# Layer 1's attention scores as three float32r products of 64 rows, two heads on the two halves of the array, in place of stacked parts

## The chip, the cores and the metric

The kernel runs on one core of a Trainium2 chip. The metric is the device time of one execution in microseconds, the lower the better. The engines are TensorE (PE in the profile, its weight loads PEld), VectorE (DVE), ScalarE (ACT), GpSimd (POOL) and SyncE (SP), which here issues the weight transfers.

## The reference, cut to what matters

Four blocks run over 256 tokens of width 1024: layer 0 (two kinds of attention, then an MLP), layer 1 (forgetting attention, then an MLP), an mLSTM mixer and a sparse-attention mixer. The change touches the forgetting attention, 16 heads of 64:

```python
def forgetting_attention(q, k, v, log_f):
    c = jnp.cumsum(log_f, axis=1)
    ...
        s = jnp.einsum("bqhd,bshd->bhqs", qb, k).astype(jnp.float32) * scale
        s = s + jnp.transpose(cq, (0, 2, 1))[..., None] - c_k[:, :, None, :]
        s = jnp.where((key_pos[None, :] <= t[:, None])[None, None], s, -jnp.inf)
        p = jax.nn.softmax(s, axis=-1)
        return jnp.einsum("bhqs,bshd->bqhd", p.astype(v.dtype), v)
```

The term of the query position cancels in the softmax, so the kernel adds only the term of the key position, `-c`.

## The kernel before, in words

**Precision.** A float32 value is cut into a high part, rounded to float32r (ACT writes it), and a low part, the remainder (DVE writes it). A product is then three float32r products: high by high, high by low, low by high. The weights are cut the same way as they arrive from memory (`cut`, L118 on ACT and L121 on DVE), and the big products are L174 to L176 (tokens on the output's partitions) and L213 to L216 (features on the partitions).

**Layer 1** (`layer1`) works in two groups of eight heads. For each it makes q, k and v (`gemm_tok`), normalises each head (`head_norm`), transposes q and k two head pairs at a time (L382) into a tile `t`, and hands four pairs to `causal_heads`. The products of the second group's q, k, v stand in the program behind the first group's attention, and the first half of `out_proj` behind the second group's, so that TensorE has other products to do while a softmax runs.

**Stacked parts.** With 64 features a head fills half of the 128 rows that a product sums over. `stack_queries` puts a head's high part on its own half of the partitions and its low part on the other half. `stack_keys` makes two arrangements of each key head, so that two products of 128 rows (L468) hold all four products of parts. A stacked head takes five instructions on TensorE: two products for each of the two blocks of query rows (128 and 256 keys wide), and one of 384 columns (L482) that adds `-c`, held as high and low rows in `negc`. Each head has a PSUM bank of its own (`banks`; two buffers of one bank).

**Layer 0** computes its scores with plain float32 operands of 64 rows: head 0 of a pair lies on partitions 0 to 63, head 1 on 64 to 127, and the products of the two alternate. Its two banks are one tile with one buffer, from the pool `p0`, which closes when layer 0 ends; the pool `pr` with the two separate banks opens then.

**Softmax** (`softmax`): four reads of the score banks by DVE (L425, two for each head), the exponentials on ACT (L428), the scaling on DVE (L443). Then TensorE transposes the weights (L455), copies follow (L457), and `pv` multiplies by v (L491). A pair's scores are asked for before the pair ahead of it is finished.

**Order.** The order of each engine's instructions is laid down by a planner when the program is built; only inside a `manual_schedule` block does TensorE keep the order as written. At run time an engine takes its instructions in that order, each waiting for its semaphores, and everything behind it on that engine waits too.

Of the kernel before, what the change touches and what calls it, by code (L numbers as in the profile page):

```python
# [16 lines left out]
P = 128  # L17
# [22 lines left out]
class Cols:  # L40
# [11 lines left out]
    def fill(self, arrays):  # L52
        out = np.zeros((P, self.n), np.float32)
        for k, a in arrays.items():
# [8 lines left out]
CST = Cols(ident=128, causal=256, mlmask=256, gmask=32, gsum=16, gsum2=48, cc=32, ss=32, cmp=30, any=2, rmask=8,  # L63
           sel=16)
# [11 lines left out]
class Builder:  # L76
# [384 lines left out]
    def scores(self, qs, kss, extra=None):  # L461
# [3 lines left out]

        def one(e, c, t0, w):
            for i, k in enumerate(kss[e]):
                nc.tensor.matmul(ss[e][:, c:c + w], qs[e][:, t0:t0 + P], k[:, :w], start=c == 0 and i == 0,  # L468
                                 stop=extra is None and c > 0 and i == len(kss[e]) - 1)

        places = ((0, 0, P), (P, P, 2 * P))
        if len(kss[0]) == 1:
            with self.tc.manual_schedule(engines={PE}):
                for place in places:
                    for e in range(2):
                        one(e, *place)
        else:
            for e in range(2):
                for place in places:
                    one(e, *place)  # L480
                if extra is not None:
                    nc.tensor.matmul(ss[e][:, :384], extra[e][0], extra[e][1], start=False, stop=True)  # L482
# [11 lines left out]
    def causal_heads(self, pool, qk, v, vcol, tables, yh, yl, npair, extra=None, sinks=None):  # L494
        def weights(p):
            pairs = [qk(p, e) for e in range(2)]
            s = self.scores([q for q, _ in pairs], [ks for _, ks in pairs],
                            [extra(2 * p + e) for e in range(2)] if extra else None)
# [14 lines left out]
    def layer0(self):  # L513
        nc, tc = self.nc, self.tc
        hg = VEC(self.vec, "hg")
        with tc.tile_pool(name="l0", bufs=2) as pool:
# [14 lines left out]
            half = lambda t, e: t[64 * e:64 * e + 64]  # L531
# [17 lines left out]
            self.causal_heads(pool, lambda p, e: (half(qT[:, 4 + p], e), [half(kT[:, 4], e)]), kv, lambda p, e: 128 + e * 64,  # L549
# [7 lines left out]
            self.causal_heads(pool, lambda p, e: (half(qT[:, p], e), [half(kT[:, p], e)]), v, lambda p, e: (2 * p + e) * 64,  # L557
# [5 lines left out]
    def layer1(self):  # L563
        nc, tc = self.nc, self.tc
        hg = VEC(self.vec, "hg")
        with tc.tile_pool(name="l1", bufs=2) as pool:
# [8 lines left out]
            nc.vector.memset(negc.bitcast(F32), 0.0)  # L575
            causal = CST(self.cst, "causal")

            def forget():
                row = self.rstd_row()
                parts = gates()  # L580
                o = self.pa.tile([P, 512], F32, name="t", tag="t", bufs=PSUM["t"])[:16, :T]
                nc.tensor.matmul(o, CST(self.cst, "gsum"), parts, start=True, stop=True)
                f = pool.tile([16, T], F32, name="f", tag="f", bufs=1)
                a = pool.tile([16, T], F32, name="fa", tag="fa", bufs=1)
                nc.vector.tensor_tensor(f, o, row[:16], op=ALU.mult)
                nc.vector.tensor_scalar(f, f, VEC(self.vec, "bf")[:16], None, op0=ALU.add)
                self.log_sigmoid(f, a)
                one = pool.tile([16, T], F32, name="fone", tag="fone", bufs=1)
                nc.vector.memset(one, 1.0)
                c = pool.tile([16, T], F32, name="fc", tag="fc", bufs=1)  # L590
# [735 lines left out]
```

## Time and profile before

| | us |
|---|---|
| three runs, median (lowest to highest) | 950.76 (949.65 to 953.34) |
| the profiled execution | 949.85 |
| its span of instructions | 947.7 |
| PE busy | 929.6 |
| DVE busy | 701.0 |
| ACT busy | 567.4 |

Busy time is the sum of the instruction records of an engine within the span. A record of TensorE lasts longer than the step to the next one, since products are pipelined, so the start-to-start step tells what an instruction takes of the engine, and a short gap does not show as idle time. The 2.1 us between the execution's time and its span lie around the instructions.

### The profile page before, as it was taken

To read this page: it belongs to the slowest core of one execution; us is meant where nothing else is said; L and a number is where in the kernel's file an instruction comes from. 1 tells how busy PE (TensorE), PEld (TensorE's weight loads), DVE (VectorE), ACT (ScalarE), POOL (GpSimd) and SP (SyncE) were. 2 spreads that over 40 slices of the span, in tenths; PEclk is the share of its full clock that TensorE was granted. 3 is DMA by queue.
4 is the path that set the end of the run, shared out by engine and by line. 5 is a ranking of instruction groups with operands and counts; after the bars stand their busy time and mean duration, and the time that the engine had idled before them with its cause. 6 is when DMAs were issued, how large, how long until landed. Compare 5 with 4: busy or idle time off the path is not lost.

```text
span 947.7 us, 17580 instructions
## 1 busy us (share of the span) xinstructions
PE 929.6 (98%) x7068; PEld 850.6 (90%) x7068; DVE 701.0 (74%) x1521; ACT 567.4 (60%) x1048; POOL 6.8 (1%) x16
## 2 busy tenths in 40 slices
PE   8999999999999999999999999999999999999997
PEld 6777999999998778899999999999888998888986
DVE  6997866655556897998665555988688778678994
ACT  7767655543445786865554444555645456379883
POOL 0000000000000000000000000000000000000000
PEclk9999999999999999999999999999999999999999
DMA  8723555555655334265555555545221555341311
GB/s 306 295 93 132 180 184 198 193 179 185 208 187 185 129 117 149 86 225 181 200 199 180 200 199 189 185 151 187 91 90 46 178 192 178 134 178 46 112 46 44
DMA packets 22608, 152.52 MB, mean 161 GB/s; under 512 B 2608, under 2 KB 2736, under 8 KB 4992
## 3 DMA queue, kind: packets, MB, share of 16 engines
q1 hardware_dynamic: 21744, 148.43, 44.9%
q0 software_dynamic: 784, 2.98, 0.9%
q8 instruction: 55, 0.90, 0.4%
q14 instruction: 25, 0.20, 0.1%
HBM read 150.36 MB, written 1.05 MB: 160 GB/s over the span
## 4 chain that ended last, share of the span: by engine, by line
PE 85%; ACT 7%; DVE 5%; issue 1%; DMA 1%; SPq 0%; ACTq 0%; DVEq 0%
PE g L213 19%; PE g L215 19%; PE g L216 19%; PE g L174 4%; PE g L175 3%; PE g L176 3%; PE o L491 2%; PE t L455 2%; ACT whi L118 2%; DVE wlo L121 1%; PE s L1058 1%; ACT kst L409 1%; DVE kst L411 1%; PE s L468 1%; PE o L828 1%
## 5 line engine op out<-in xcount | busy, mean ns | idle before, releaser
L121 DVE TENSOR_TENSOR wlo<-wraw,whi 128x1024 fp32r<-128x1024 f32 (+1 forms) x274 | 324.3, 1203 | 138.3 <-ACT whi L118 137.7
L118 ACT ACTIVATE whi<-wraw 128x1024 fp32r<-128x1024 f32 (+1 forms) x274 | 277.9, 1041 | 222.6 <-PE g L215 121.6
L213 PE MATMUL g<-xh,whi 128*128 128x256 f32 x928 | 260.9, 281 | 0.4 <-ACT nqr L1010 0.4
L216 PE MATMUL g<-xh,wlo 128*128 128x256 f32 x928 | 261.0, 281 | 0.0
L215 PE MATMUL g<-xl,whi 128*128 128x256 f32 x928 | 260.6, 281 | 0.5 <-DVE xl L254 0.5
L213 PEld LDWEIGHTS g<-xh,whi 128*128 128x128 f32 x928 | 174.4, 188 | 4.1 <-issue 3.0
L216 PEld LDWEIGHTS g<-xh,wlo 128*128 128x128 f32 x928 | 175.7, 189 | 0.6
L215 PEld LDWEIGHTS g<-xl,whi 128*128 128x128 f32 x928 | 174.6, 188 | 1.2 <-DVE xl L254 0.7
L216 PE MATMUL g<-hh,wlo 128*128 128x256 f32 x512 | 141.5, 276 | 0.0
L213 PE MATMUL g<-hh,whi 128*128 128x256 f32 x512 | 141.5, 276 | 0.0
L215 PE MATMUL g<-hl,whi 128*128 128x256 f32 x512 | 141.3, 276 | 0.0
L213 PEld LDWEIGHTS g<-hh,whi 128*128 128x128 f32 x512 | 96.1, 188 | 0.0
L215 PEld LDWEIGHTS g<-hl,whi 128*128 128x128 f32 x512 | 96.1, 188 | 0.0
L216 PEld LDWEIGHTS g<-hh,wlo 128*128 128x128 f32 x512 | 96.1, 188 | 0.0
L174 PE MATMUL g<-whi,xh 128*128 128x512 f32 x192 | 76.4, 399 | 2.4 <-DVE E L929 1.6
L175 PE MATMUL g<-wlo,xh 128*128 128x512 f32 x192 | 75.9, 395 | 0.0
L176 PE MATMUL g<-whi,xl 128*128 128x512 f32 x192 | 75.7, 396 | 0.0
L216 PE MATMUL g<-yh,wlo 128*128 128x256 f32 x224 | 63.3, 283 | 0.0
L213 PE MATMUL g<-yh,whi 128*128 128x256 f32 x224 | 63.2, 284 | 0.0
L215 PE MATMUL g<-yl,whi 128*128 128x256 f32 x224 | 63.2, 283 | 0.0
L428 ACT ACTIVATE L<-L,nm 128x128 f32<-128x128 f32 (+1 forms) x128 | 56.8, 450 | 6.8 <-DVE nm L425 6.5
L174 PEld LDWEIGHTS g<-whi,xh 128*128 128x128 f32 x192 | 36.1, 188 | 12.8 <-ACT xh L253 2.6
(348 smaller groups left out, 1396.7 us busy)
## 6 DMA issues: line engine op xcount, KB each, us to landing
wraw<-in_w SPq DMA_DIRECT2D x135, 1024.0 KB, 4.9
wraw<-in_w SPq DMA_DIRECT2D x4, 512.0 KB, 7.3
tabs<-in_tabs SPq DMA_DIRECT2D x2, 1024.0 KB, 8.3
xT<-in_x SPq DMA_DIRECT2D x4, 256.0 KB, 7.4
bdv<-in_bdv POOLq DMA_DIRECT2D x8, 128.0 KB, 4.7
mlw<-in_mlw POOLq DMA_DIRECT2D x1, 992.0 KB, 5.2
nq<-in_gf POOLq DMA_DIRECT2D x1, 512.0 KB, 6.6
out_y<-nqr SPq DMA_DIRECT2D x2, 256.0 KB, 2.1
```

The source lines that it names most:

```text
L118: self.nc.scalar.activation(hi[:, s], w[:, s], AF.Copy)
L121: self.nc.vector.tensor_tensor(lo[:, s], w[:, s], hi[:, s].bitcast(F32), op=ALU.subtract)
L174: nc.tensor.matmul(ps[b][:, :n], xh, hi[:, sl], start=kt == 0, stop=False)
L175: nc.tensor.matmul(ps[b][:, :n], xh, lo[:, sl], start=False, stop=False)
L176: nc.tensor.matmul(ps[b][:, :n], xl, hi[:, sl], start=False, stop=kt == KT - 1)
L213: nc.tensor.matmul(o, hi[:, s], ah, start=bank["new"], stop=False)
L215: nc.tensor.matmul(o, hi[:, s], al, start=False, stop=False)
L216: nc.tensor.matmul(o, lo[:, s], ah, start=False, stop=last and j == 1 and i == len(acts) - 1)
L409: nc.scalar.activation(dst[64 * o:64 * o + 64, :, e, o], ps[own], AF.Copy, scale=sc)
L428: nc.scalar.activation(Ls[i][:, c], Ls[i][:, c], AF.Exp, bias=nm[:, b, i:i + 1], scale=-1.0, accum_out=den[:, b, i:i + 1])
L455: nc.tensor.transpose(ps[:, e, j * P:(j + 1) * P], Ls[e][:, i * P:(i + 1) * P], self.ident)
L491: nc.tensor.matmul(o[64 * e:64 * e + 64, kt * P:T], v[:, kt, c0[e]:c0[e] + 64], pts[kt][:, e], start=start and kt == 0, stop=stop and kt == 1)
```

## The change

Layer 1 no longer stacks. `to_parts` writes the high part of a transposed q or k with one ACT instruction over 128 partitions and the low part with one DVE instruction. `scores` takes a list of terms, for layer 1 (high q, low k), (low q, high k), (high q, high k), and for layer 0 the one float32 term as before. For every term it issues the products of 64 rows of head 0 and head 1 in turn, then one product of 384 columns and 64 rows for each head that adds `-c`, all in one `manual_schedule` block. The product of the two low parts, which the stacked form had, is left out.

The forget gates are computed on 128 partitions, four copies of 16 rows, instead of 16, so that both halves of the partitions hold the high and the low rows of `c`. Layers 0 and 1 and both their MLPs now run inside the pool `p0`, so layer 1 gets the one tile of two banks; `pr` opens before the mLSTM.

```diff
-    def scores(self, qs, kss, extra=None):
+    def scores(self, terms, extra=None):
         nc = self.nc
         ss = self.banks()
...
+        half = lambda t, e: t[64 * e:64 * e + 64]
+        with self.tc.manual_schedule(engines={PE}):
+            for i, (q, k) in enumerate(terms):
+                for c, t0, w in ((0, 0, P), (P, P, 2 * P)):
                     for e in range(2):
+                        nc.tensor.matmul(ss[e][:, c:c + w], half(q, e)[:, t0:t0 + P], half(k, e)[:, :w],
+                                         start=c == 0 and i == 0, stop=extra is None and c > 0 and i == len(terms) - 1)
+            if extra is not None:
+                for e in range(2):
+                    nc.tensor.matmul(ss[e][:, :384], half(extra[e][0], e), half(extra[e][1], e), start=False, stop=True)
         return [(s[:, :P], s[:, P:384]) for s in ss]
...
+    def to_parts(self, dst, t, c0, scale=None):
+        nc = self.nc
+        ps = self.transposed(t, c0, dst.shape[2])
+        hi = dst[:, 0].bitcast(F32)
+        if scale is None:
+            self.split(dst[:, 0], dst[:, 1], ps)
+        else:
+            nc.scalar.activation(dst[:, 0], ps, AF.Copy, scale=scale)
+            nc.vector.scalar_tensor_tensor(dst[:, 1], ps, scale, hi, op0=ALU.mult, op1=ALU.subtract)
...
-            nc.vector.memset(negc.bitcast(F32), 0.0)
+            gsum = pool.tile([P, P], F32, name="gsum", tag="gsum", bufs=1)
+            nc.vector.tensor_copy(gsum.rearrange("p (a b) -> p a b", b=32),
+                                  CST(self.cst, "gsum").unsqueeze(1).to_broadcast([P, 4, 32]))
...
+                hi = pool.tile([P, T], F32R, name="fhi", tag="fhi", bufs=1)
+                nc.scalar.activation(hi, c, AF.Copy, scale=-1.0)
                 for a, w in ((0, P), (P, T)):
-                    nc.scalar.activation(negc[:16, a:a + w], c[:, :w], AF.Copy, scale=-1.0)
-                    nc.vector.scalar_tensor_tensor(negc[32:48, a:a + w], c[:, :w], -1.0, negc[:16, a:a + w].bitcast(F32),
-                                                   op0=ALU.mult, op1=ALU.subtract)
+                    nc.vector.scalar_tensor_tensor(negc[:, a:a + w], hi[:, :w].bitcast(F32), CST(self.cst, "lorow"), c[:, :w],
+                                                   op0=ALU.mult, op1=ALU.add)
...
-                    self.stack_queries(qst[-1], q, p * P)
-                    kst.append(late(pool, [2, 2, 2, T], f"kst{p}"))
-                    self.stack_keys(kst[-1], k, p * P, gk)
+                    self.to_parts(qs[-1], q, p * P)
+                    ks.append(late(pool, [2, 2, T], f"kst{p}"))
+                    self.to_parts(ks[-1], k, p * P, gk)
+                def terms(p):
+                    (qh, ql), (kh, kl) = ([t[p // 2][:, i, p % 2] for i in range(2)] for t in (qs, ks))
+                    return [(qh, kl), (ql, kh), (qh, kh)]
...
             with tc.tile_pool(name="p0", bufs=1, space=bass.MemoryType.PSUM) as self.p0:
-                self.layer0()
+                for s in (self.layer0, lambda: self.mlp(2), self.layer1, lambda: self.mlp(4)):
+                    s()
             with tc.tile_pool(name="pr", bufs=2, space=bass.MemoryType.PSUM) as self.pr:
-                for s in (lambda: self.mlp(2), self.layer1, lambda: self.mlp(4), self.mlstm, self.nsa):
+                for s in (self.mlstm, self.nsa):
```

## Rows read from the trace of the kernel before

**Rows 1.** The page's busy times: us, share of the span, instructions.

```profile
PE 929.6 (98%) x7068; PEld 850.6 (90%) x7068; DVE 701.0 (74%) x1521; ACT 567.4 (60%) x1048; POOL 6.8 (1%) x16
```

**Rows 2.** Windows: length, then busy us (instructions) of PE, PEld, DVE, ACT, POOL.

```profile
36.00:70.50 34.50, 34.50 (x198) 25.60 (x197) 32.01 (x100) 24.91 (x63) 0.00 (x0) 1.00 0.36 125
70.50:110.00 39.50, 38.54 (x318) 34.05 (x317) 31.79 (x87) 28.91 (x73) 0.00 (x0) 1.00 0.42 141
300.00:321.00 21.00, 21.00 (x106) 16.35 (x105) 15.66 (x34) 13.93 (x21) 0.00 (x0) 1.00 0.29 100
321.00:357.00 36.00, 33.55 (x194) 25.66 (x193) 32.70 (x82) 31.16 (x68) 0.00 (x0) 1.00 0.42 147
372.00:405.00 33.00, 31.36 (x250) 28.03 (x249) 30.36 (x81) 26.72 (x63) 0.00 (x0) 1.00 0.36 129
```

**Rows 3.** Timeline of TensorE in layer 1: start, us, instructions, idle time before.

```profile
324.74 0.39 PE L175 MATMUL g<-wlo,xh 128*128 128x512 f32 x1
325.71 0.33 PE L468 MATMUL s<-kst,qst 128*128 128x128 f32 x1 [0.58 <-DVE kst L411]
...
334.84 0.39 PE L175 MATMUL g<-wlo,xh 128*128 128x512 f32 x1
336.04 0.70 PE L468 MATMUL s<-kst,qst 128*128 128x128 f32 x4 [0.81 <-DVE nm L425]
...
336.76 0.62 PE L468 MATMUL s<-kst,qst 128*128 128x128 f32 x4
337.21 0.34 PE L482 MATMUL s<-negc,selr 128*128 128x384 f32 x1
337.38 0.39 PE L176 MATMUL g<-whi,xl 128*128 128x512 f32 x1
...
401.95 0.28 PE L215 MATMUL g<-yl,whi 128*128 128x256 f32 x1
402.26 0.87 PE L491 MATMUL o<-pt,v 128*64 128x256 f32 x8
```

**Rows 4.** Groups by line and shape, 285 to 413 us: count | busy, mean ns | idle before.

```profile
L411 DVE SCALAR_TENSOR_TENSOR kst<-t,gk,kst 64x512 fp32r<-64x512 f32 x16 | 12.0, 749 | 2.3 <-ACT kst L409 1.9
L409 ACT ACTIVATE kst<-t,gk 64x512 fp32r<-64x512 f32 x16 | 10.9, 683 | 1.0 <-PE t L382 0.7
...
L468 PE MATMUL s<-kst,qst 128*128 128x128 f32 x32 | 6.7, 280 | 2.7 <-DVE nm L425 1.9 <-DVE kst L411 0.8
...
L425 DVE CUSTOM_DVE_ANT_0 L<-s,cst 128x256 f32<-128x256 f32 x16 | 6.6, 415 | 0.0
...
L398 DVE TENSOR_TENSOR qst<-t,qst 64x512 fp32r<-64x512 f32 x8 | 5.5, 689 | 0.3
...
L397 ACT ACTIVATE qst<-t 64x512 fp32r<-64x512 f32 x8 | 4.7, 590 | 0.9 <-DVE qst L398 0.8
L301 DVE TENSOR_TENSOR xT<-g,xT 128x512 f32<-128x512 f32 x7 | 4.6, 675 | 1.5 <-PE g L216 1.5
```

**Rows 5.** The tile qT in layer 0: duration in ns, min/median/max.

```profile
L388 ACT ACTIVATE qT<-t x4: 590/602/622, 38.9 to 73.3; 128x512 f32<-128x512 f32 x4
```

**Rows 6.** TensorE's waits from 30 to 108 us, layer 0: us, times, longest.

```profile
PE t L455 <- DVE L L443: 0.8, 2, 0.6
```

**Rows 7.** Timeline of TensorE around one pair's scores in layer 0.

```profile
42.24 0.39 PE L176 MATMUL g<-whi,xl 128*128 128x512 f32 x1
42.47 0.40 PE L174 MATMUL g<-whi,xh 128*128 128x512 f32 x1
42.80 0.93 PE L468 MATMUL s<-kT,qT 64*128 64x128 f32 x8
43.66 0.50 PE L175 MATMUL g<-wlo,xh 128*128 128x512 f32 x1
44.00 0.40 PE L176 MATMUL g<-whi,xl 128*128 128x512 f32 x1
```

**Rows 8.** The same timeline cut to 42.79 to 42.82 us.

```profile
42.80 0.38 PE L468 MATMUL s<-kT,qT 64*128 64x128 f32 x2
```

More of the change, by code (lines that the diff above doesn't have):

```diff
@@ L495, in weights @@
         def weights(p):
-            pairs = [qk(p, e) for e in range(2)]
-            s = self.scores([q for q, _ in pairs], [ks for _, ks in pairs],
-                            [extra(2 * p + e) for e in range(2)] if extra else None)
+            s = self.scores(qk(p), [extra(2 * p + e) for e in range(2)] if extra else None)
             kw = {}
@@ L580, in forget @@
                 parts = gates()
[L581 to L586, printed above, removed]
+                o = self.pa.tile([P, 512], F32, name="t", tag="t", bufs=PSUM["t"])[:, :T]
+                nc.tensor.matmul(o, gsum, parts, start=True, stop=True)
+                f = pool.tile([P, T], F32, name="f", tag="f", bufs=1)
+                a = pool.tile([P, T], F32, name="fa", tag="fa", bufs=1)
+                nc.vector.tensor_tensor(f, o, row, op=ALU.mult)
+                nc.vector.tensor_scalar(f, f, VEC(self.vec, "bf"), None, op0=ALU.add)
                 self.log_sigmoid(f, a)
[L588 removed]
+                one = pool.tile([P, T], F32, name="fone", tag="fone", bufs=1)
                 nc.vector.memset(one, 1.0)
[L590 removed]
+                c = pool.tile([P, T], F32, name="fc", tag="fc", bufs=1)
                 nc.vector.tensor_tensor_scan(c, one, f, 0.0, op0=ALU.mult, op1=ALU.add)
+                hi = pool.tile([P, T], F32R, name="fhi", tag="fhi", bufs=1)
+                nc.scalar.activation(hi, c, AF.Copy, scale=-1.0)
                 for a, w in ((0, P), (P, T)):
[L593 to L595 removed]
+                    nc.vector.scalar_tensor_tensor(negc[:, a:a + w], hi[:, :w].bitcast(F32), CST(self.cst, "lorow"), c[:, :w],
+                                                   op0=ALU.mult, op1=ALU.add)
             def extra(h0):
@@ L610, in layer1 @@
                 v = self.tok_evac(pool, self.gemm_tok(), "v", bufs=2)
-                qst, kst = [], []
+                qs, ks = [], []
                 for p in (0, 2):
-                    qst.append(pool.tile([P, 2, 2, T], F32R, name="qst", tag=f"qst{p}", bufs=1, align_bytes=LINE))
-                    self.stack_queries(qst[-1], q, p * P)
-                    kst.append(late(pool, [2, 2, 2, T], f"kst{p}"))
-                    self.stack_keys(kst[-1], k, p * P, gk)
-                self.causal_heads(pool, lambda p, e: (qst[p // 2][:, p % 2, e],
-                                                      [kst[p // 2][:, p % 2, e, o] for o in range(2)]), v,
+                    qs.append(pool.tile([P, 2, 2, T], F32R, name="qst", tag=f"qst{p}", bufs=1, align_bytes=LINE))
+                    self.to_parts(qs[-1], q, p * P)
[4 more added lines that the diff above has]
+                    return [(qh, kl), (ql, kh), (qh, kh)]
+                self.causal_heads(pool, terms, v,
                                   lambda p, e: (2 * p + e) * 64, lambda h: causal,
@@ L1248, in layout, with rows16 @@
     two = lambda v: np.concatenate([v, v])[:, None]
+    def rows16(v):
+        out = np.zeros((4, 32, v.shape[1]))
+        out[:, :16] = v
+        return out.reshape(P, -1)
     allp = lambda v: np.broadcast_to(v[None], (P,) + v.shape)
```

36 lines of the change are left out of this document (8 added, 28 removed).

## Prediction

> **What bounds the kernel now.** I read the busy times first. TensorE is busy for 929.6 of 947.7 us [rows 1], so a change pays if it shortens TensorE's own sequence or closes one of its gaps; work saved on DVE or ACT alone is worth nothing. Next I cut the trace into windows around both layers' attention and compared TensorE's busy time with the length. Layer 1's two stretches lack 36.00 - 33.55 = 2.45 and 33.00 - 31.36 = 1.64 us. Layer 0's, with as much softmax and as many pairs, lack 0 and 0.96 us [rows 2]. The idle column understates it, because a record outlasts its step. So I went through the steps from start to start. A 512-column product steps by 0.23 us, but from 324.74 to 325.71 it is 0.97: 0.74 lost, waiting for the key parts (kst, L411). From 334.84 to 336.04 it is 1.20: 0.97 lost, waiting for DVE to read a score bank (L425) [rows 3]. There are 18 such places in the two stretches, the first at 324.74 and the last at 401.95, where 0.31 less 0.12 for a 256-column product and 0.10 for going over to the narrow products of `pv` leaves 0.09 lost. They add up to 3.8 us in the first stretch and 2.7 in the second, 6.5 in all.
>
> The grouped lines say what DVE and ACT do there. In the two stretches L411 and L398 take 12.0 + 5.5 = 17.5 us of DVE, L409 and L397 10.9 + 4.7 = 15.6 us of ACT. They share the engines with the reads of the banks; the idle time before L468 is put down to exactly these two, 1.9 us to nm and 0.8 to kst [rows 4].
>
> **Cutting the parts.** For two pairs the old code issues 2 + 4 ACT instructions and 2 + 4 DVE instructions of 64x512; the new one 2 and 2 of 128x512. Twice the partitions cost nothing more by the nearest rows: on ACT 602 ns for 128x512 against 590 for 64x512, on DVE 675 against 689 [rows 4, 5]. Four times (two pairs, twice in each group) that is ACT 4 x (0.59 + 0.68) = 5.1 us in place of 15.6 and DVE 4 x (0.69 + 0.75) = 5.8 in place of 17.5. So 10.5 us of ACT and 11.7 of DVE go from 69 us of stretches in which DVE was busy for 32.70 + 30.36 = 63.1 [rows 2]. That buys only what TensorE waited for. Waits on kst and qst should nearly vanish, since q and k are each ready one ACT and one DVE instruction after their transposes. The bank reads get in sooner, too: behind two L411 they came 1.5 us late. What is late next is the softmax itself, as in layer 0, where the only wait listed is two times, 0.8 us, for the scaled weights [rows 6]; by my count from start to start layer 0 loses 1.7 us. I take layer 1 to fall to that level: 6.5 - 1.7 = 4.8 us gained. Bounds: 2.6 us if just the seven losses on kst and qst go, 6.5 if all go.
>
> **The products.** A stacked head takes 0.45 us for four products and 0.17 for `-c`, from 336.76 to 337.38, so a pair takes 1.24 [rows 3]. The new pair has seven products on each half: 2 x 3 of 128 and 256 columns and the one of 384. If both halves run abreast, that is one old head and two more products at 0.45 / 4 = 0.11: 0.62 + 0.22 = 0.84 us. To this comes the change-over between whole and half array. Layer 0 shows it: 42.47 to 42.80 is 0.33 against 0.23, and 43.66 to 44.00 is 0.34 against 0.23, so at least 0.10 + 0.11 = 0.21. At most, the whole detour of 42.47 to 44.00 less two steps, 1.53 - 0.46 = 1.07, is overhead except for four records of a half at 0.11: 0.63 [rows 7]. The new pair costs 1.05 to 1.47 against 1.24, for eight pairs 1.5 us gained to 1.8 lost. No row has float32r on half an array. I take the middle, 0, since next to `pv` one change-over serves both and elsewhere the planner may break a block in two.
>
> That the halves run abreast is seen in layer 0: in the 0.02 us around 42.80 two products are under way, one of each head [rows 8].
>
> **The rest.** The gates work on the same number of elements per partition, with one ACT instruction fewer, no memset of `negc`, a copy more and wider weights. This ends before 321, where TensorE is busy for 21.00 of 21.00 us [rows 2]: nothing, and without that cover 1.2 us, two instructions of the size of those in [rows 5]. The constants grow by 17 columns in a transfer of layer 0; I put nothing. `p0` living on gives layer 1 one tile for both heads: that is the first rival.
>
> **The sum.** 949.85 - 4.8 + 0 = 945.05 for an execution like the profiled one, which lies 0.91 below the median of the runs; by that median it would be 945.96. I predict 945.5. What a measurement of this kernel can tell from no change is about 0.5%, 4.75 us, so the likeliest case lies on that edge.
>
> **Rivals.**
>
> *The block waits for two banks.* Before, head 0 of the next pair could start when its own bank had been read. Now fourteen products stand in one block behind four reads, and every big product queued behind them waits along. The second head's two reads add up to twice 0.42 = 0.83 us [rows 4]. Six pairs follow another one in their group. Three of them now lose 0.97, 0.95 and 0.47; with 0.7 of that more for all six, about 1.5 each, it is 9 us in place of 2.4, and 2.6 of the other waits go: +4.0, 953.9 us. It ends above the old time once the six wait more than (2.4 + 2.6) / 6 = 0.8 us each. Against it: layer 0 has this tile and this block, and no wait of L468 [rows 6]. For it: the planner's order is new, and layer 0 has no low parts to write.
>
> *Only the key waits go.* The freed time doesn't help the softmax chain: 2.6 us gained, 947.3.
>
> *Weight loads do not hide within a half.* A product on half the array waits for its own load, 0.11, since the pitch of 0.11 is the same for 128 and 256 columns and so is the load's. Then a half takes 7 x 0.11 + 3 x 0.05 + 3 x 0.11 + 0.17 = 1.42, with the least change-over 1.63, 0.4 more than 1.24: 8 x 0.4 = 3.2 lost, 948.3 us. Against it: on the whole array 384 columns step by 0.17, three quarters of the 0.23 for 512, so there loads cost nothing [rows 3, 7].
> The rule behind this rival is in the Trainium skill, TensorE: Matmul & The Clock Gate, Part 3 (Packing small matmuls): a weight load overlaps a running product only where the two use different row groups. By that rule the sum is this rival's 948.3, by the row 945.05; the whole-array row does not agree with it, and no row here has float32r on 64 rows.
>
> *The heads run one after another.* Twelve products at 0.11, two at 0.17 and 0.21 make 1.87 a pair, 0.63 more: 5.0 lost, 950.1 us. Against it stands [rows 8].
>
> **Chances.** The forecast 0.60, with a range of its own from 942 (6.5 of waits and 1.5 of products gained) to 948 (3.5 gained and 1.8 lost); only the key waits 0.14; loads not hidden 0.10; one after another 0.05; two banks 0.11. The range should leave out 2 in 10: 942 at the lower end, 951 at the upper, which leaves out the dearer part of the two-bank case and the edges of the forecast. Faster by over 0.5% needs nearly the full 4.8: a little over half of the forecast's 0.60, and a bit from the key waits, 0.36. Slower by over 0.5% is the tail of the two banks, 0.08. The rest, 0.56, is no change that can be told.
>
> **What would show it.** Right: L468 in layer 1 with 64 rows and start times in couples; eight blocks of 0.8 to 1.0 us from first to last start; idle time of TensorE in the two stretches 1.0 to 1.5 us in place of 4.1; DVE some 6 us less in each; L411 and L398 gone. Wrong: waits of L468 on nm of over 0.8 us each (two banks); starts in a half 0.2 apart (loads); no couples (one after another); blocks torn apart by other work, each piece paying its change-over; or stalls that appear behind 405 us, where the code is unchanged but the order may not be.

## The result and the profile after

The changed kernel takes 955.76 us (median of 14 runs, 953.2 to 960.92) against 949.93 (14 runs, 946.75 to 953.78) on the same chip: a ratio of 1.0069, with a 95% interval of 1.0052 to 1.0086. It is slower by 0.7%, where I had forecast 945.5 us and had given "slower" 0.08.

The page's busy times of the changed kernel, the answer to [rows 1]:

```profile
PE 932.6 (98%) x7100; PEld 853.6 (90%) x7100; DVE 691.5 (73%) x1507; ACT 554.3 (58%) x1029; POOL 6.8 (1%) x16
```

DVE and ACT did lose work, 9.5 and 13.1 us. TensorE is busy for 3 us more. To see where, I read the first start of each stage in both traces and subtracted. The two profiled spans are 947.7 and 952.6 us, 4.9 apart:

| stretch | before, us | after, us | difference |
|---|---|---|---|
| layer 0 and its output product, to 107.6 / 108.8 | 107.6 | 108.8 | +1.2 |
| first MLP | 178.3 | 178.3 | 0 |
| layer 1 with its output product, where the change works | 125.6 | 125.0 | -0.6 |
| second MLP | 175.8 | 181.8 | **+6.0** |
| mLSTM and its output product | 212.6 | 210.7 | -1.9 |
| sparse attention | 147.8 | 148.0 | +0.2 |

The first row belongs to a stretch at the start: from 9.4 to 12.9 us the granted clock is 0.51 in the changed kernel's profile, the lower level of 1.2 GHz, after TensorE had been busy for 3.31 of the 5.40 us ahead of it (5.12 in the kernel before, which stays at 1.00). In another execution of the changed kernel (e2 below), without this fall, the row ends at 107.1. So layer 1 gained next to nothing in these two profiles, and the loss lies in the second MLP, whose code is the same.

**Layer 1.** Windows of the changed kernel, columns as in [rows 2], the stretches of layer 1's attention:

```profile
321.00:357.00 36.00, 32.37 (x207) 23.92 (x206) 28.39 (x77) 23.51 (x58) 0.00 (x0) 1.00 0.32 118
372.00:405.00 33.00, 31.33 (x270) 27.15 (x269) 28.29 (x77) 19.85 (x54) 0.00 (x0) 1.00 0.36 128
```

TensorE lacks 3.63 and 1.67 us, against 2.45 and 1.64 in [rows 2], though DVE has 6.4 us less to do. Counted from start to start as in the prediction, the waits were 6.5 us and are about 6.6. TensorE's waits of the changed kernel from 285 to 430 us (us, times, longest):

```profile
PE s L482 <- DVE nm L436: 1.6, 2, 0.9
PE t L382 <- DVE qst L144: 1.5, 1, 1.5
PE t L466 <- DVE L L454: 1.2, 2, 0.6
PE o L495 <- ACT pt L468: 0.6, 1, 0.6
```

The same names as before in a new order: bank reads (nm), one low part (qst), scaled weights (L). The longest is seen in two timelines. TensorE of the changed kernel:

```profile
324.83 0.39 PE L174 MATMUL g<-whi,xh 128*128 128x512 f32 x1
326.76 0.66 PE L382 MATMUL t<-cst,q 128*128 128x128 f32 x4 [1.54 <-DVE qst L144]
...
327.48 0.60 PE L382 MATMUL t<-cst,k 128*128 128x128 f32 x4
328.02 0.95 PE L482 MATMUL s<-kst,qst 64*128 64x128 f32 x12
328.81 0.34 PE L486 MATMUL s<-negc,selr 64*128 64x384 f32 x2
329.08 0.50 PE L176 MATMUL g<-whi,xl 128*128 128x512 f32 x1
329.42 0.39 PE L174 MATMUL g<-whi,xh 128*128 128x512 f32 x1
```

And DVE of the changed kernel at the same place:

```profile
321.48 4.63 DVE L121 TENSOR_TENSOR wlo<-wraw,whi 128x1024 fp32r<-128x1024 f32 x4
326.02 0.69 DVE L144 TENSOR_TENSOR qst<-t,qst 128x512 fp32r<-128x512 f32 x1
```

The low part of q is one short instruction now, as planned, but it stands behind four cuts of weights (L121) and starts at 326.02; the transposes that need its bank come at 326.76. The first timeline also shows the new block: twelve products and two of `-c`, 1.06 us from 328.02 to 329.08. The two change-overs lie outside these 1.06: the last of the four transposes ahead of the block steps by 0.20 in place of 0.11, and from 329.08 to 329.42 it is 0.34 in place of 0.23. With them a block costs 1.26 us, against 1.24 for an old pair.

**The second MLP.** Windows over exactly this stage, first the kernel before, which [rows 2] do not show:

```profile
411.50:587.30 175.80, 175.33 (x1546) 175.14 (x1546) 114.02 (x135) 89.57 (x117) 0.53 (x1) 1.00 0.57 199
```

The changed kernel:

```profile
412.10:593.90 181.80, 181.80 (x1547) 181.80 (x1546) 112.59 (x133) 87.93 (x113) 0.53 (x1) 1.00 0.55 193
```

The same products, the full clock in both, no waits in the new one and 0.47 us of them in the old: the products themselves are slower. Grouped lines of 40 us in the middle of the upward half (430 to 470 us; count, busy us, mean ns) say how. The kernel before:

```profile
L215 PE MATMUL g<-xl,whi 128*128 128x256 f32 x119 | 32.8, 276 | 0.0
```

The changed kernel:

```profile
L213 PE MATMUL g<-xh,whi 128*128 128x256 f32 x114 | 32.0, 281 | 0.0
```

119 of a line's products fit into 40 us there, 114 here. From start to start a product takes 113.3 ns there (three steps in 340) and 117.8 here (nine in 1060), hardly varying through the whole stretch. In 768 products, one half of an MLP, that is 768 x 4.43 = 3.4 us. Both halves of the second MLP run at 117.8: +6.8, less what the old kernel loses there to a late DVE. Two of its steps are longer than 0.11, by 0.63 and 0.11 us, 0.74 together:

```profile
415.85 0.28 PE L215 MATMUL g<-xl,whi 128*128 128x256 f32 x1
416.59 0.39 PE L215 MATMUL g<-xl,whi 128*128 128x256 f32 x1 [0.47 <-DVE xl L254]
416.81 0.28 PE L216 MATMUL g<-xh,wlo 128*128 128x256 f32 x1
```

That makes 6.1 us; 6.0 were measured.

### The profile page after: what moved, and what is told of

It reads as the page before. It is cut to its first block, busy times and chain, and to the rows that moved or that the text cites. A ratio compares the mean times of both kernels' runs of the same rounds, so it can differ in the third digit from the quotient of the medians.

```text
span 952.6 us, 17597 instructions
## 1 busy us (share of the span) xinstructions
PE 932.6 (98%) x7100; PEld 853.6 (90%) x7100; DVE 691.5 (73%) x1507; ACT 554.3 (58%) x1029; POOL 6.8 (1%) x16
## 3 DMA queue, kind: packets, MB, share of 16 engines
HBM read 150.36 MB, written 1.05 MB: 159 GB/s over the span
## 4 chain that ended last, share of the span: by engine, by line
PE 88%; DVE 6%; ACT 4%; issue 1%; DMA 1%; SPq 0%; ACTq 0%; DVEq 0%
PE g L213 19%; PE g L215 19%; PE g L216 19%; PE g L174 4%; PE g L175 4%; PE g L176 4%; PE o L495 2%; PE t L466 2%; DVE wlo L121 2%; PE s L1068 1%; ACT L L439 1%; PE s L482 1%; PE o L838 1%; PE s L824 1%; PE s L810 1%
## 5 line engine op out<-in xcount | busy, mean ns | idle before, releaser
L121 DVE TENSOR_TENSOR wlo<-wraw,whi 128x1024 fp32r<-128x1024 f32 (+1 forms) x274 | 324.6, 1205 | 141.8 <-ACT whi L118 141.4
L216 PE MATMUL g<-hh,wlo 128*128 128x256 f32 x512 | 144.0, 281 | 0.0
L213 PE MATMUL g<-hh,whi 128*128 128x256 f32 x512 | 144.0, 281 | 0.0
L215 PE MATMUL g<-hl,whi 128*128 128x256 f32 x512 | 143.9, 281 | 0.0
L213 PEld LDWEIGHTS g<-hh,whi 128*128 128x128 f32 x512 | 98.3, 192 | 0.0
L213 PE MATMUL g<-yh,whi 128*128 128x256 f32 x224 | 63.1, 282 | 0.0
L216 PE MATMUL g<-yh,wlo 128*128 128x256 f32 x224 | 63.1, 282 | 0.0
```

What stands on the lines that cost most here:

```text
L121: self.nc.vector.tensor_tensor(lo[:, s], w[:, s], hi[:, s].bitcast(F32), op=ALU.subtract)
L213: nc.tensor.matmul(o, hi[:, s], ah, start=bank["new"], stop=False)
L215: nc.tensor.matmul(o, hi[:, s], al, start=False, stop=False)
L216: nc.tensor.matmul(o, lo[:, s], ah, start=False, stop=last and j == 1 and i == len(acts) - 1)
```

## The experiments

Times are medians, with lowest and highest; ratios are to the kernel before, run beside on the same chip (949.7 to 951.6 us there), with their 95% intervals. First all runs of whole kernels, with the mean step of TensorE's 256-column products in each half of both MLPs of the profiled execution (ns, start to start, steps over 170 left out):

| run | us | ratio | first MLP up, down | second MLP up, down |
|---|---|---|---|---|
| before, changed (first profiles) | | | 117.8, 113.4; 113.3, 117.8 | 113.3, 113.4; 117.8, 117.8 |
| e1 before again | 951.15 (945.8 to 957.7) | 1.0008 [0.9971, 1.0044] | 113.3, 113.4 | 113.3, 113.4 |
| e2 changed again | 953.65 (949.4 to 958.0) | 1.0037 [1.0003, 1.0072] | 113.3, 113.4 | 117.8, 117.8 |
| e3 pool only | 952.68 (945.7 to 959.8) | 1.0029 [0.9992, 1.0066] | 117.8, 117.8 | 117.6, 113.4 |
| e4 separate banks | 955.48 (951.4 to 963.9) | 1.0071 [1.0036, 1.0107] | 113.3, 113.4 | 117.8, 117.8 |
| e5 parts first | 956.40 (950.3 to 963.0) | 1.0064 [1.0033, 1.0095] | 113.3, 113.4 | 117.8, 117.8 |
| e6 late residual | 958.03 (951.7 to 963.9) | 1.0077 [1.0040, 1.0115] | 117.8, 113.4 | 113.7, 117.8 |
| e7 narrow break | 954.25 (950.8 to 961.8) | 1.0049 [1.0016, 1.0083] | 113.3, 117.8 | 117.8, 117.8 |
| e9 before, shifted | 955.71 (951.8 to 960.8) | 1.0048 [1.0022, 1.0074] | 113.3, 117.8 | 113.4, 117.8 |
| e10 changed, aligned | 954.84 (946.2 to 959.3) | 1.0030 [0.9996, 1.0064] | 117.8, 113.4 | 117.8, 113.3 |
| e13 two breaks | 951.22 (948.9 to 954.0) | 0.9989 [0.9960, 1.0019] | 117.8, 113.4 | 113.6, 113.4 |
| e14 four breaks | 947.85 (946.4 to 952.0) | 0.9949 [0.9924, 0.9975] | 113.4, 113.4 | 113.6, 114.5 |
| e15 aligned, one break | 946.73 (942.9 to 956.8) | 0.9948 [0.9912, 0.9983] | 113.3, 113.4 | 113.6, 117.8 |
| e16 before, 64 bytes | 954.01 (947.4 to 960.4) | 1.0017 [0.9983, 1.0052] | 117.8, 117.8 | 117.6, 117.8 |
| e17 aligned, four breaks | 945.68 (943.6 to 948.2) | 0.9943 [0.9913, 0.9974] | 113.3, 113.4 | 113.6, 114.4 |
| e18 before, four breaks | 949.14 (945.7 to 951.8) | 0.9977 [0.9948, 1.0006] | 113.6, 113.4 | 113.6, 113.4 |

**Both kernels again, and the two-bank tile.** e1 and e2 are the two kernels unchanged. e3 is the old kernel with the new life of the tile pools, e4 the new one with the old:

```diff
# e3, on the kernel before
-                self.layer0()
+                for s in (self.layer0, lambda: self.mlp(2), self.layer1, lambda: self.mlp(4)):
+                    s()
# e4, on the changed kernel: the reverse
```

> The kernel before, unchanged, once more. Theory A (the step of the MLP's products, 113 or 118 ns, is settled by chance in each execution): ratio 1.000 within 0.3%, but in its profile at least one of the six long stretches of products (up and down in both MLPs, the mLSTM's, its output) has the other step than in the first profile (118, 113, 113, 113, 117, 118 ns). Theory B (the program's order settles it): the same six steps again.

> The changed kernel, unchanged, once more. Theory A (chance settles the 113 or 118 ns step): its four MLP stretches are not again 113, 118, 118, 118 ns, and the 5 to 6 us that the first profile loses in the second MLP are not found there; the ratio stays at 1.005 to 1.009 only if something else, the clock's start or layer 1, loses it. Theory B (settled by the program): 113, 118, 118, 118 again, ratio 1.006 to 1.008. Both: layer 1 as in the first profile, 6.6 us of TensorE's waits, within 1 us of the old stretch.

> The kernel before with only the two-bank tile: the pool p0 lives on to the end of the second MLP, the scores stay stacked. If the one tile for both heads is what eats the gain (the rival of the two banks), waits on the bank reads grow: 6 following pairs lose 0.5 to 1 us each more, ratio 1.003 to 1.007. If it is of no account, as layer 0 let expect, ratio within 0.998 to 1.002 and waits of L468 on nm stay at about 2 us.

> The changed kernel with two separate banks in layer 1 (the pool pr opens after layer 0 as before). If the one tile costs the time, this gives it back: 3 to 6 us less than the changed kernel, ratio to before 0.998 to 1.003. If the block of fourteen products waits for both banks in any case, and the rest lies elsewhere, the ratio stays at 1.005 to 1.009 and the two long waits on nm of about 0.9 us are still there.

The two-bank tile is not the loss: without it the changed kernel stays at 1.0071. The pool alone is unclear (1.0029, the interval reaches below 1). Either edit also makes the planner order layer 1 anew (the layer takes 127.2 us in e3 and 126.1 in e4), so the two do not price the tile by itself. Of the step, e1 and e2 are the cleanest pair, since their first MLPs agree: layer 1 takes 125.7 and 124.9 us, the second MLP 175.8 and 181.9. The step differs between executions of one program, but in the second MLP the changed kernel had 117.8 in both its profiles (and e4 in its own) and the kernel before 113.3 in both (e3 begins at 113.3 too, and has 117.8 from a wait at 420 us to the end of the upward half).

**Layer 1's waits.** e5 moves the cutting of the parts ahead of v's product:

```diff
-                v = self.tok_evac(pool, self.gemm_tok(), "v", bufs=2)
                 qs, ks = [], []
                 for p in (0, 2):
                 ...
+                v = self.tok_evac(pool, self.gemm_tok(), "v", bufs=2)
```

> The changed kernel with q's and k's parts cut ahead of the product that makes v, so that VectorE has them in hand before that group's next weight cuts. Theory A (layer 1's waits only moved to the parts, which stand behind three weight cuts on VectorE): the two waits of transposes for the low parts (1.9 us at 324.8 and what answers to it in the other half) go, TensorE's waits in layer 1 fall from 6.6 to 3-4 us, the time is 2-3 us under that of the changed kernel, about 1.003 of the kernel before. Theory B (the planner fills the place with other work, as it did when the stacking went): waits stay at 6-7 us and the time stays within 1 us of the changed kernel, 1.005 to 1.007. Neither theory touches the second MLP, where a product should keep its 118 ns.

Theory A failed: the wait for qst went, as it said, but others took its place. TensorE's waits in e5:

```profile
PE t L466 <- DVE L L454: 2.9, 2, 2.3
PE s L482 <- DVE nm L436: 1.6, 2, 0.9
PE t L382 <- DVE q L372: 1.5, 1, 1.5
```

They come to 6.0 us, against 4.9 in the changed kernel. Layer 1 took 127.9 us from the end of the first MLP to the second, 2.9 more than in the changed kernel; about half of that is a stretch with the granted clock at 0.51 (329.2 to 332.6 us). Theory B, that the order fills the gap with other work, stands.

**A break ahead of the second MLP.** e6 delays DVE so that TensorE has to wait there, as it did in the old kernel; e7 puts a small product in:

```diff
# e6, in residual
+        if gi == 3 and n0 == 6:
+            for _ in range(4):
+                nc.vector.tensor_scalar(x, x, 1.0, None, op0=ALU.mult)
# e7, in mlp, ahead of the second group
+                if gi_next == 4 and n == 1:
+                    nc.tensor.matmul(o[:64, :64], self.xT[:, 7, :64], self.xT[:, 7, :64], start=True, stop=True)
```

> The changed kernel with four more VectorE passes over the last two tiles of layer 1's residual (times 1.0, in place), which makes VectorE late by about 2 us at the start of the second MLP, as it was in the kernel before, so that TensorE has to wait there. Theory A (TensorE's step of 256-column products is set at a break and then held; the changed kernel lost the break at the head of the second MLP): the wait costs 1-2 us, the step of the second MLP falls from 117.8 to 113.3 ns, which gives back 6.8 us over 1536 products: 4 to 6 us under the changed kernel, 0.999 to 1.003 of the kernel before. Theory B (the step is settled otherwise, by chance or by the stage's data and addresses): 1-2 us slower than the changed kernel, 1.006 to 1.009, and 117.8 ns as often as before.

> The changed kernel with one product of 64 rows by 64 columns, which nobody reads, put between the first and second group of the second MLP: a break in TensorE's row of like products without a wait for another engine. Theory A (any break lets the step be set anew): a step of 113.3 ns behind it in some or all executions, 3 to 6 us under the changed kernel, 0.999 to 1.003 of the kernel before. Theory B (only a real wait sets the step): 117.8 ns on both sides of the product and the changed kernel's time, 1.004 to 1.007.

In e6's profile the upward half has 113.7 ns and the downward half again 117.8: behind the wait the step is lower, and only to the end of that half. It cost 2.1 us of wait, and the ratio of 1.0077 is no lower than the changed kernel's, so as a cure it failed. e7 has 117.8 on both sides of its break: not every break moves the step.

**The products by themselves.** e8, e11 and e12 leave all layers out and run only the MLP's own sequence of products, with breaks between blocks (`columns`: two one-column products of full precision, as the norm makes them).

> All layers are left out. After the first weights have come, 50 blocks of 48 products of 256 columns (the MLP's own sequence of weights and moving tiles), and behind each block one of ten breaks, five times over: none, two single-column products, four products of 64 columns, four of 128 columns in four passes, four float32r products of 64 rows, two float32r products of 128 and of 192 columns, a wait for one and for two ScalarE reads of a bank, one product of 64 by 64. Theory A (two held steps): every block has one step throughout, near 113 or near 118 ns, no block lies between the two, the block behind no break keeps its forerunner's step, and breaks differ in which step follows. Theory B (the step goes with a stage's data, tiles or transfers): all 50 blocks have the same step, since they share all of these.

> All layers are left out, as in the run of breaks alone, whose 50 blocks all had 120.0 ns a product, not 113.3 or 117.8. There the weights' parts lay at an offset of 48 elements in their tiles, as the moving tiles do. Here 20 blocks of 48 products have weights at offsets of 0 to 112 elements (twice over), then 14 blocks at offset 0 have seven kinds of break behind them, then 6 blocks have VectorE and ScalarE at work on other tiles, at aligned and unaligned places. Theory A (the step is set by where weights and moving tiles lie): 113.3 ns at offset 0 and 120.0 ns at offset 48, the same in both passes and behind any break. Theory B (a state that a break sets): different steps at one offset, by the break before it. If VectorE's and ScalarE's work at unaligned places slows the products, the last three blocks show it against the three before.

> All layers are left out, as in the run of offsets alone; weights lie at offset 0, where that run had either 113.4 or 117.8 ns a product, held through a block. Here every tested break has a block of known step before it (four full-precision products of 64 columns lead to 113, two float32r products of 192 columns to 118, as in that run) and a block behind it, twice over with blocks of 48 and of 72 products ahead of it. Tested: two single-column products with their operands at 0, 32, 64 and 96 bytes past a line of 256; one to four full-precision products of 64 columns, one of 32, one of 128. Theory A (what the break reads, and where it lies, sets the step behind it): one step for each break, and the single-column break gives 113 at aligned places and 118 at 96 bytes. Theory B (the step before is carried over): the step behind a single-column break is that of the block before it, at all four places. Theory C (only the moment counts): steps differ between the two passes of one and the same break.

e8 was a miss for both theories in one respect: all of its blocks had about 120 ns (119.7 to 120.9), whatever the break. e11 gives the reason. With weights at an offset of 48 elements it has 119.9 again; other offsets give, in both passes alike, 117.8 at 0, 32 and 64, 117.4 at 8, 118.7 at 16, 119.8 at 24, 116.8 at 40, 118.3 at 56 and 119.7 at 112. So the step depends on where weights lie, at least behind the one kind of break that these twenty blocks had. But at offset 0 the later blocks of e11 had 113.4 to 113.8 or 117.8 to 118.2, with the break before them. ScalarE at work beside the last blocks changed nothing, at aligned or unaligned places (117.8 throughout); VectorE's part ran only behind them, so that its contention wasn't tried.

e12 tests the breaks. Its 79 blocks behind the first (48 or 72 products each, weights at offset 0) have one of the two steps, means of 113.4 to 114.1 or of 117.7 to 118.2 ns, none between. What each break made of the step before it:

| break | in, out (times) |
|---|---|
| two float32r products of 192 columns | 113 to 118 (11), 118 to 113 (9) |
| one full-precision product of 64 columns, of 128; three of 64 | step kept (12 of 12) |
| one of 32 columns; two of 64 | 118 to 113 (8 of 8); none stood behind 113 |
| four of 64 | 113 to 118 (14), 118 to 113 (7), 118 to 118 (2) |
| `columns` at 96 bytes | 113 to 118 (4 of 4) |
| `columns` at 0 bytes | 113 to 118 (1), 118 to 113 (2) |
| `columns` at 32 bytes | 118 to 113 (3), 113 to 113 (1) |
| `columns` at 64 bytes | 118 to 113 (2), 118 to 118 (2) |

None of the three theories is right as it stood: what the step becomes depends on the break, on the step before and on the place of the operands. The windows of e12 over one such series, each inside a block (start to end, length, PE busy and its count first), show the step alternate: 44, 46, 45, 46 records in 5 us, behind a product of 32 columns (122.10), two of 192 (127.90) and one of 32 (133.70):

```profile
116.20:121.20 5.00, 5.00 (x44) 5.00 (x44) 0.00 (x0) 0.00 (x0) 0.00 (x0) 1.00 0.00 0
122.10:127.10 5.00, 5.00 (x46) 5.00 (x46) 0.00 (x0) 0.00 (x0) 0.00 (x0) 1.00 0.00 0
127.90:132.90 5.00, 5.00 (x45) 5.00 (x44) 0.00 (x0) 0.00 (x0) 0.00 (x0) 1.00 0.01 3
133.70:138.70 5.00, 5.00 (x46) 5.00 (x46) 0.00 (x0) 0.00 (x0) 0.00 (x0) 1.00 0.00 0
```

**Where the tiles lie.** The change adds 17 columns to the table of constants, which pushes x's parts up by 256 bytes and tiles without an asked-for alignment by 96. e9 does that to the old kernel and nothing else, but for one product of layer 0 that the planner then puts 3 us earlier; e16 adds 16 columns and moves the same product; e10 gives the changed kernel its alignment back:

```diff
# e9 (pad=16 in e16), on the kernel before
-           sel=16)
+           sel=16, pad=17)
# e10, on the changed kernel
-           sel=16, lorow=1)
+           sel=16, lorow=1, pad=47)
```

> The kernel before with 17 unused columns in the table of constants, as many as the change adds to it: the tiles kept through the whole kernel, the ring of weights in part and the MLP's tiles then lie where the changed kernel has them (x's parts 256 bytes higher, the tiles that ask for no alignment 96 bytes higher, no longer at multiples of 64); nothing else differs. Theory A (the loss outside layer 1 comes from these addresses): 954 to 956 us, 1.004 to 1.007 of the kernel before, second MLP at 117.8 ns a product. Theory B (it comes from the order and timing of the work, or from chance): within 0.25% of the kernel before, second MLP at 113.3 ns.

> The changed kernel with 47 more unused columns in the table of constants, so that every tile that is kept lies exactly 256 bytes above its place in the kernel before and has its alignment back. Theory A (addresses): 948 to 951 us, 0.998 to 1.001 of the kernel before, second MLP at 113.3 ns. Theory B (order and timing): the changed kernel's time, 1.004 to 1.007, second MLP at 117.8 ns.

> The kernel before with 16 unused columns in the table of constants, not 17: tiles lie 64 bytes higher, still at multiples of 64, and x's parts 256 bytes higher, as with 17. Theory A (the alignment lost by the 17th column makes the downward half slow): the kernel before's time, 0.998 to 1.002, downward half at 113.3 ns. Theory B (any shift, or the place of x's parts): 1.003 to 1.007, as with 17 columns, downward half at 117.8 ns.

Seventeen unused columns make the old kernel slower by 0.5%, without one instruction changed and at the same mean clock (0.997), so two thirds of the loss can come from places. The two halves of e9's second MLP in the profile (430 to 470 and 530 to 570 us):

```profile
L213 PE MATMUL g<-xh,whi 128*128 128x256 f32 x119 | 32.8, 276 | 0.0
...
L213 PE MATMUL g<-hh,whi 128*128 128x256 f32 x114 | 32.0, 281 | 0.0
```

The step changes between the halves, at the four passes of the norm's one-column products. But neither theory of e9 to e16 holds as a rule: e16's second MLP has 117.8 ns in both halves of its one profile (from a wait at 419.7 us on) at a time of 1.0017, and e10, aligned, lies between the kernels. Places may shift the odds of a step; they do not fix it.

**Setting the step by hand.** In e12 a full-precision product of 32 columns led from 118 to 113 each of the four times. It takes 0.14 us, and the product behind it 0.20 in place of 0.11, so it costs 0.23. e13 puts one behind the first group of each half of the second MLP, e14 of both MLPs; e15 is e10 with one in the upward half of the second; e17 is e10 and e18 the old kernel with all four. TensorE's order is otherwise that of the kernel it is put into (in e18 one product moved by a dozen places).

```diff
+    def one_small(self):
+        o = self.pa.tile([P, 512], F32, name="t", tag="t", bufs=PSUM["t"])
+        self.nc.tensor.matmul(o[:, :32], self.ident, self.ident[:, :32], start=True, stop=True)
# in mlp, up and down
+                if n == 1 and gi_next in (4,):
+                    self.one_small()
```

> The changed kernel with two full-precision products of 128 rows by 32 columns that nobody reads, one behind the first of the 16 groups of the second MLP's upward half, one behind the first of the 4 groups of its downward half; TensorE's order is otherwise the same and addresses too. In the run of entries and breaks such a product (32 columns) cost 0.14 us and had 113.3 ns behind it each of the 4 times that 117.8 ns stood before it. Theory A (the held step is the loss): both halves at 113.3 ns from there on, 6.4 us less, 948 to 950 us, 0.998 to 1.000 of the kernel before. Theory B (the loss lies elsewhere, the step is only seen beside it): the changed kernel's time, 1.004 to 1.007.

> The same with two more such products in the first MLP, whose step differs from execution to execution in both kernels. Theory A, if the product only ever turns 118 into 113: 2 to 4 us under the run with two breaks, 0.994 to 0.998 of the kernel before, and less spread. If it turns 113 into 118 as well: as the run with two breaks on the mean. Theory B: 1.004 to 1.007.

> The changed kernel with 47 more unused columns of constants (its downward half of the second MLP had 113.3 ns in that run, its upward half 117.8) and one such product in the upward half only. Theory A (order makes the upward half slow, addresses the downward half): both at 113.3 ns, 3 us under the aligned kernel, 0.998 to 1.001 of the kernel before. Theory B: the aligned kernel's time, 1.003.

> The changed kernel with 47 more unused columns of constants and a product of 32 columns in each half of both MLPs. The four breaks alone gave 947.9 us, a spread of 2 us in 11 of 12 runs, and the aligned kernel with one break 942.9 to 956.8 us. Theory A (a break sets the step to 113.3 ns wherever 117.8 ns stood before it): 944 to 948 us, 0.992 to 0.996 of the kernel before, spread of some 2 us. Theory B (the product flips the step either way): as with one break or worse, 947 to 953 us, wide spread.

> The kernel before with a product of 32 columns in each half of both MLPs. Theory A (the breaks set the step; the change itself gives the 0.6 us that layer 1's stretch shows): 944 to 949 us, 0.993 to 0.997 of the kernel before, and 0 to 2 us above the changed kernel with the same breaks and alignment. Theory B (the change itself costs or gives more than layer 1's stretch shows): the two differ by over 3 us.

Theory A's ratio came in e13 (0.9989), and the loss of 0.7% was gone with two products of 0.23 us, at the changed kernel's clock (0.996 in the mean of its runs, two falls inside layer 1 in its profile). The line shown above for both kernels, 430 to 470 us, reads in e13:

```profile
L215 PE MATMUL g<-xl,whi 128*128 128x256 f32 x119 | 32.8, 276 | 0.0
```

In the profiles of e13, e14, e15, e17 and e18 such a product found 117.8 eight times and had 113.3 behind it each time (once beside a wait, in e18); seven times it found 113.3 and left it. The timeline of e17 around one of them; the three products ahead of it start 0.12 apart, those well behind it 0.11 to 0.12:

```profile
519.47 0.28 PE L213 MATMUL g<-hh,whi 128*128 128x256 f32 x1
519.59 0.28 PE L215 MATMUL g<-hl,whi 128*128 128x256 f32 x1
519.71 0.28 PE L216 MATMUL g<-hh,wlo 128*128 128x256 f32 x1
519.82 0.30 PE L324 MATMUL t<-cst 128*128 128x32 f32 x2
519.96 0.36 PE L213 MATMUL g<-hh,whi 128*128 128x256 f32 x1
520.16 0.28 PE L215 MATMUL g<-hl,whi 128*128 128x256 f32 x1
```

Two decimals hardly show it; 18 us on either side do. Groups of e17 by line and shape, 499 to 517 and 522 to 540 us:

```profile
L213 PE MATMUL g<-hh,whi 128*128 128x256 f32 x52 | 14.6, 281 | 0.0
...
L213 PE MATMUL g<-hh,whi 128*128 128x256 f32 x54 | 14.9, 276 | 0.0
```

Here one product turns 117.8 into 113.3 inside a stretch, with the same tiles and the same lines on either side; in e15, without that product, this half keeps 117.8 to its end. e14 and e17 have a narrow spread and beat both kernels: 947.85 and 945.68 us, 0.9949 [0.9924, 0.9975] and 0.9943 [0.9913, 0.9974]. e15 reached the lowest times of all, 942.9, but goes up to 956.8; in its profile the half without a break has 117.8. Its expectation, that alignment alone keeps the downward half at 113.3, failed there.

With the same breaks, and tiles aligned in both, the changed kernel (e17) has a mean 3.2 us below the old one (e18), twice its standard error being 1.5. That is on the side that I had forecast, but the profiles put little of it into layer 1, which takes 125.8 us in e18 and 126.2 in e17, or 125.0 without the fall of the clock (e14, the same order). 3.1 us of the two profiles' 4.2 lie in the first 72 us, where e18's granted clock falls to 0.53 from 8 to 12 us, behind 1.98 busy of 4.00; this does not belong to the change. Nor does the clock make the 3.2 of the means: over the twelve runs it is 0.997 in e17 and 0.998 in e18. What does stays open.

**The clock in layer 1.** The two first profiles do not show a second, smaller part of the loss. Falls of the granted clock to 0.50 turned up inside layer 1 in seven of the eleven profiles of the changed kernel and its variants (e5, e6, e7, e15 and e17 once, e10 and e13 twice), and in none of the six of the kernel before and its variants. Where the changed kernel's order of layer 1 is kept, this layer takes 124.9 to 125.0 us without a fall (three profiles), 126.2 to 126.4 with one and 127.8 to 127.9 with two. Two windows of e17, columns as in [rows 2], show one:

```profile
375.50:379.50 4.00, 2.48 (x24) 1.86 (x23) 3.54 (x18) 1.86 (x8) 0.00 (x0) 1.00 0.77 272
379.50:382.90 3.40, 3.40 (x18) 2.83 (x18) 2.58 (x12) 2.13 (x9) 0.00 (x0) 0.50 0.00 0
```

TensorE had waited ahead of it (2.48 us busy of 4.00). In the changed kernel's first profile it is busy for 2.41 of 4.00 us from 380 to 384, and the clock stays at 1.00, so the fall doesn't come each time. The clock averaged over whole runs says the same: 0.995 in the changed kernel's 14 runs and 0.996 in e2's 12, against 0.997 to 0.998 in the runs of the kernel before beside the experiments. The difference is about 0.002; of 950 us that is 1 to 2 us of the 5.8 measured, an estimate. No experiment here keeps the clock up, so this part is seen, not tested.

## Why the prediction was wrong

- **What bounds the kernel** was right: TensorE, 98% in both. But the prediction reads a gap in TensorE's row as the only place where time can be lost there. A full row can lose 6 us as well.
- **Cutting the parts** was right in the work: four instructions of 128x512 each for q and k on ACT and DVE, 0.69 to 0.75 us on DVE as taken; DVE lost 6.4 of its 63.1 us in the two stretches, ACT and DVE 13.1 and 9.5 in all.
- **"I take layer 1 to fall to that level: 6.5 - 1.7 = 4.8 us gained" is the step of the sum that failed.** The waits are 6.6 us. They hang on when DVE comes to an instruction, not on how much it has to do: qst's low part waits behind four cuts of weights (321.48 to 326.02), and the planner that orders them laid the freed time elsewhere. e5 moved the low parts forward and got other waits, 6.0 us by name against 4.9. My own lower bound, 2.6, was too high; a bound below which "the planner spends it" would lie was missing.
- **The products** were put at 0, between 1.5 gained and 1.8 lost. A whole block takes 1.06 us without its change-overs and 1.26 with them, the middle of 1.05 to 1.47: the term was right. The 1.06 lie nearer to the 0.84 of hidden loads than to the 1.42 of loads that do not hide, and far from 1.66 for heads in turn (1.87 less 0.21), so heads do run abreast and loads hide in the main; both rivals on this fall. Four of the eight blocks are torn apart by `pv` (335.94 and 337.16, for one) and take 1.26 to 1.37 us in their two pieces, as the text feared. By these two terms layer 1 should gain nothing; it gains 0.6 us without a fall of the clock and loses as much with one. What the 0.6 are, I did not find.
- **The block waits for two banks**, the rival on the slow side: its waits are there, but smaller (1.6 us in two places against 1.9 in three for nm), far from its 9 us. The kernel is slower for another reason.
- **"The constants grow by 17 columns in a transfer of layer 0; I put nothing"** is the term that was missing. Their transfer shows no cost (layer 0 ends at 107.0 us in e9's profile, at 107.6 and 107.4 in the two of the kernel before), but they move tiles, and e9, which adds only them and moves one product, took 0.5% longer. What the runs showed in place of nothing is 6.8 us on the second MLP's 1536 products, which hold the other step; the columns may tip it, and so may the changed order ahead. No row of mine priced the step of unchanged products as something that a change could alter, though both steps stood in the trace of the kernel before (first MLP up 117.8, second 113.4).
- **The clock** stands in no term at all: the new waits of layer 1 come with falls of the granted clock in seven of eleven profiles, at 1.2 to 1.5 us each.

Shown: the held step is the larger part of the loss (e13 against the changed kernel, both with the same tiles and, but for two products, the same order). Only argued: what tips it in the second MLP. For the upward half the profiles speak for the order ahead: all eleven of the changed kernel and its variants enter the second MLP at 117.8 ns, aligned or not (e10, e15, e17), and five of the six of the kernel before and its variants at 113.3, shifted or not (e9, e16); e18, with its breaks, is the exception. The downward half follows no such rule: e9 speaks for places there, e15 and e16 against them.

## What to carry to other kernels

When a change moves the time by under 1%, compare the step of products that it did not touch, stage by stage, before explaining anything by the change itself; count a line's records in equal windows of both traces. Work taken from a side engine pays only if the order on that engine brings the late instruction forward; ask what stands ahead of it. And where a long run of like products sets the time, try one small product as a break in it: here four of 0.23 us brought the changed kernel from 1.0037 or 1.0069 to 0.9949 and narrowed the spread to 5 or 6 us (14 in the kernel before on e17's chip), but gained the kernel before only 0.2%, which its interval does not tell from nothing (e18).

## What the runs showed of the hardware

- A run of float32r products of 128 rows and 256 columns, each with its own weights, has two steps at one and the same clock, 113.3 and 117.8 ns, and keeps the one it has until a break: for up to 768 products in the kernel, in all 79 blocks of e12.
- The break decides in part by its kind: one product of 64 columns kept the step (4 of 4), one of 32 turned 118 into 113 (4 of 4, and 8 of 8 in the kernel, where it left 113 as it was 7 of 7 times), two float32r products of 192 turned either into the other (20 of 20). Others did not act alike each time: behind four products of 64, 118 became 113 seven times and stayed twice. Why, no run here shows.
- With weights at other offsets in their tile the step lies between 116.8 and 119.9 ns; at 48 elements, where the moving tiles lie too, no break brought it under 119.7 (e8).
- The granted clock fell to 0.50, the lower level, in layer 1 (329.2 to 332.6 us in e5, 379.5 to 382.9 in e17), behind stretches with TensorE busy for 1.21 of 3.50 us and 2.48 of 4.00; after 2.41 of 4.00 in the changed kernel's first profile it stayed at 1.00. One such fall cost layer 1 1.2 to 1.5 us.
